# A hybrid pool-mixer and mLSTM block: right sums of the output projections made one pass earlier and in place, first operands of the projections split inside the mLSTM, weight loads separated from their split, head norm in groups of two tiles

## The chip, the cores and the metric

The kernel runs on one core of one Trainium2 chip. A core has a matrix engine (TensorE, PE in the profile; PEld is its weight load), VectorE (DVE), ScalarE (ACT), GpSimd (POOL) and SyncE (SP), which issues most of the transfers. Each engine takes its instructions in the order of the program. Times are device microseconds of one execution; before the change the median of three runs is 3157.75 us (3157.44 to 3160.65).

## The reference

Everything is float32; the sequence has 4096 rows, and D_MODEL, both groups' widths and the output are 1024 columns wide.

```python
def reference(x, norm_w, w_in, ...):
    u = rmsnorm(x, norm_w[l])
    proj = u @ w_in[l]                       # 1024 x 5120
    pool_x, pool_z, m_x, m_z, m_o = ...      # five slices of 1024
    y_pool = pool_mixer(pool_x, pool_w[l], pool_scale[l]) * jax.nn.silu(pool_z)
    y_mlstm = mlstm_branch(m_x, m_z, m_o, ...)
    mixed = jnp.concatenate([y_pool, y_mlstm], axis=-1)
    x = x + mixed @ w_out[l]                 # 2048 x 1024
    return rmsnorm(x, final_norm_w)

def mlstm_branch(mx, mz, mo, ...):
    xc = jax.nn.silu(causal_conv(mx, conv_w, conv_b))
    ...                                      # q, k, v maps, gates, chunkwise mLSTM of 4 heads
    h = jax.nn.sigmoid(mo) * h
    mu = jnp.mean(h, axis=-1, keepdims=True)             # per head, 256 columns
    var = jnp.mean(jnp.square(h - mu), axis=-1, keepdims=True)
    hn = ((h - mu) * lax.rsqrt(var + EPS)).reshape(B, S, 1024) * mh_norm_w
    return (hn + m_skip * xc) * jax.nn.silu(mz)
```

## The kernel before, in words

Every float32 product is made from two halves: `split` (L110, L111) writes a rounded high part with ACT and the rest with DVE, and `mm3` (L117, L118, L119) multiplies high by high, high by low and low by high.

**Phase A** (0 to 752.7 us) normalises 8 blocks of 512 rows, writes the result to memory (`us_d`), projects pool_x and pool_z, and writes the pool mixer's output (`yp_d`). Between the blocks' steps, at the steps that `JOBS_AT` names, `sums` (L493 loads, four POOL operations, L497 stores) makes the left sums of `us_d` and `yp_d` that phase C needs. The last pair for `yp_d` runs after the loop.

**Phase B** (to 1758.1 us) is the mLSTM, 32 chunks of 128 rows, steps ordered by the text `ORDER`. It first loads and splits its weights `wm` (L127 through two buffers `ws`) and the block-diagonal maps (L623), then for each two chunks `project` loads u (L700), casts it (L702), takes the low part (L703) and multiplies; the front part of a chunk begins with L740. Its steady state is a pair of chunks in 58.05 us. When nothing is left to project, `next_weights` takes that place: it loads and splits the right operands of the first four products of phase C.

**Phase C** is four passes driven by `drive`: pass 1 `o1` (pool output times upper half of w_out, plus x, to `r_d`), pass 2 `mo` (output gate, head norm, then 256 transposes L1069 to `hs_d`), pass 3 `mz` (the mz gate times `hs_d`, to `ym_d`), pass 4 `o2` (`ym_d` times the lower half of w_out, plus `r_d`, and the final norm). A pass works on 4 row blocks of 1024 rows. Each block is 7 products of half-size matrices in place of 8, from sums of quarters of the left and of the right matrix (Strassen's scheme in Winograd's form), each product in two steps of 24 matmuls of 128 by 512: 56 steps a pass. The seven results chain through sums in PSUM and in tiles named `ch`.

What sets the order around the change:

- Left operands: ACT's queue issues their load three steps ahead (tile `sr`), and they are split two steps ahead on ACT and DVE (`make`).
- Right operands: seven slots per pass. `Pass.load` loads and splits one; in the last row block of a pass the next pass's slots are loaded, each directly at the step where the old slot is free. The sums of quarters among them (`SUM_OF`) come from memory, where `Pass.stage` has put them (5 tiles, POOL) during earlier passes: those of passes 2 and 3 in pass 1, those of pass 4 in pass 3. For pass 1 they are made while loading (`load_right`, L129 on POOL).
- Transposes: `Head.done` normalises one tile of 128 rows by 512 columns (two heads): DVE statistics, POOL power (L1038), DVE bias (L1040), ACT scaling (L1043). The groups of four tiles are transposed at the steps that `FREE_BANKS` names, after which L1071 on DVE evicts the bank.
- Left sums of pass 4: when the last of a block's four results is there, `put_sums` (L201, L203, L205, L209 on POOL) and deferred stores (L196 on SP) follow. Pass 4's additions to `r_d` load it with L980.
- The program reuses eight completion counters in turn for transfers, so that a transfer also waits until the one eight places ahead, from SP or ACT, has landed.

## Time and profile before

| | us |
|---|---|
| median of three runs | 3157.75 |
| profiled execution, its own time | 3153.02 |
| its span, first to last instruction | 3151.3 |
| phase A | 752.7 |
| phase B, with its entry | 1005.4 |
| phase C | 1393.2 |

The page gives busy time and share of each engine, the span in 40 slices, the transfers, the chain that ended last and the costliest groups. A stretch table gives the same busy times for chosen stretches, with the clock that TensorE was granted (1.00 is full), the share of time that the 16 DMA engines were busy, and GB/s. A group's row ends with the idle time of its engine just before it and the operation that ended it. The table of waits for TensorE names that operation for every gap, with the sum, the number and the longest. Numbers in brackets with x count instructions.

### The profile page before, as it was taken

Reading aid. Unit: us, or ns where it says so; the run is one execution under the profiler, and the core shown is the slowest. Engines: PE = TensorE matmul, PEld = TensorE weight load, DVE = VectorE, ACT = ScalarE, POOL = GpSimd, SP = SyncE. Lnnn points to the kernel's source line nnn. Section 1 sums busy time; section 2 is a strip of 40 time slices with the busy share of each in tenths; the row PEclk is TensorE's granted clock in tenths of the full one; section 3 lists DMA queues with packets and bytes.
Section 4 is the critical chain, followed back from the end, with each engine's and each line's share of the span. In section 5 each row is a group of like instructions: output and inputs, shape, how many; then the busy total and the mean of one; then the engine's idle time right before and its main releaser. Section 6 shows DMA issues by size and latency. Waiting matters only on the chain. (4 is left out here: it accounts for less than half of the span.)

```text
span 3151.3 us, 45085 instructions
## 1 busy us (share of the span) xinstructions
PE 2919.7 (93%) x15912; PEld 2522.1 (80%) x15912; DVE 2089.8 (66%) x4160; ACT 1373.6 (44%) x2727; POOL 960.7 (30%) x1015
## 2 busy tenths in 40 slices
...
GB/s 211 124 153 159 155 181 184 184 174 201 46 64 51 48 68 48 61 55 51 61 58 111 227 309 268 238 225 192 209 218 230 260 273 302 260 290 208 213 208 157
DMA packets 256419, 530.55 MB, mean 168 GB/s; under 512 B 28352, under 2 KB 71872, under 8 KB 256192
## 3 DMA queue, kind: packets, MB, share of 16 engines
...
q14 instruction: 102, 0.84, 0.1%
...
## 5 line engine op out<-in xcount | busy, mean ns | idle before, releaser
L117 PE MATMUL acc<-u,w 128*128 128x512 f32 (+1 forms) x2016 | 691.6, 343 | 2.2 <-ACT u L110 1.8
L119 PE MATMUL acc<-u,w 128*128 128x512 f32 (+1 forms) x2016 | 682.4, 339 | 0.0
L118 PE MATMUL acc<-u,w 128*128 128x512 f32 (+1 forms) x2016 | 680.7, 338 | 0.0
L117 PE MATMUL ps<-w,sr 128*128 128x512 f32 x1344 | 536.7, 399 | 44.4 <-ACT sr L110 29.6
L119 PE MATMUL ps<-w,sr 128*128 128x512 f32 x1344 | 533.6, 397 | 9.2 <-DVE sr L111 9.0
L118 PE MATMUL ps<-w,sr 128*128 128x512 f32 x1344 | 532.5, 396 | 0.0
L111 DVE TENSOR_TENSOR sr<-sr 128x1024 fp32r<-128x1024 f32 x224 | 293.5, 1314 | 304.3 <-ACT sr L110 299.4
L110 ACT CAST sr<-sr 128x1024 fp32r<-128x1024 f32 x224 | 234.2, 1048 | 552.0 <-PE ps L118 293.6
L117 PEld LDWEIGHTS acc<-u,w 128*128 128x128 f32 x2016 | 383.7, 190 | 44.3 <-ACT u L110 2.5
L118 PEld LDWEIGHTS acc<-u,w 128*128 128x128 f32 x2016 | 383.7, 190 | 40.3
L119 PEld LDWEIGHTS acc<-u,w 128*128 128x128 f32 x2016 | 383.5, 190 | 40.2
L117 PEld LDWEIGHTS ps<-w,sr 128*128 128x128 f32 x1344 | 257.9, 192 | 99.6 <-ACT sr L110 32.3
L119 PEld LDWEIGHTS ps<-w,sr 128*128 128x128 f32 x1344 | 257.1, 191 | 69.5 <-DVE sr L111 16.7
L118 PEld LDWEIGHTS ps<-w,sr 128*128 128x128 f32 x1344 | 257.6, 192 | 53.5 <-issue 0.5
L656 DVE SCALAR_TENSOR_TENSOR xc<-mx,col,xc 128x256 f32<-128x256 f32 x384 | 221.2, 632 | 55.4 <-POOL mx L715 46.4
L644 POOL TENSOR_TENSOR cs<-c,cs 128x516 fp32r<-128x516 f32 x124 | 176.4, 1422 | 204.2 <-ACT cs L643 181.7
L1038 POOL TENSOR_TENSOR rs<-rs,nhalf 128x2 f32<-128x2 f32 x64 | 56.0, 876 | 521.0 <-DVE mv L1035 325.9
L117 PE MATMUL ps<-sr,w 128*128 128x512 f32 x448 | 176.5, 394 | 4.3 <-ACT sr L110 3.3
L118 PE MATMUL ps<-sr,w 128*128 128x512 f32 x448 | 176.0, 393 | 1.4 <-DVE sr L111 1.4
L119 PE MATMUL ps<-sr,w 128*128 128x512 f32 x448 | 175.7, 392 | 0.0
L867 PE MATMUL mm<-va,st 128*128 128x258 f32 x384 | 85.6, 318 | 64.2 <-DVE st L111 42.6
L322 DVE TENSOR_TENSOR ch<-ps,ch 128x512 f32<-128x512 f32 x192 | 127.2, 681 | 14.4 <-PE ps L119 13.6
...
## 6 DMA issues: line engine op xcount, KB each, us to landing
sr<-us_d ACTq DMA_DIRECT2D x112, 512.0 KB, 5.0
...
```

The lines of the kernel that those rows point to most:

```text
L110: nc.scalar.copy(out=hi, in_=raw)
L111: (eng or nc.vector).tensor_tensor(out=lo, in0=raw, in1=hi.bitcast(F32), op=ALU.subtract)
L117: nc.tensor.matmul(ps, lhsT=a[0], rhs=b[0], start=start and k == 0, stop=False, skip_group_check=skip)
L118: nc.tensor.matmul(ps, lhsT=a[0], rhs=b[1], start=False, stop=False, skip_group_check=skip)
L119: nc.tensor.matmul(ps, lhsT=a[1], rhs=b[0], start=False, stop=stop and k == n - 1, skip_group_check=skip)
L322: nc.vector.tensor_tensor(out=v(t), in0=ps, in1=v(t), op=ALU.add)
L644: nc.gpsimd.tensor_tensor(out=t[:, 1], in0=cst[h], in1=t[:, 0].bitcast(F32), op=ALU.subtract)
L656: nc.vector.scalar_tensor_tensor(out=a[:, t], in0=m[:, t, i:i + TB], scalar=conv_w[:, jj * 4 + i:jj * 4 + i + 1], in1=a[:, t], op0=ALU.mul ...
L867: nc.tensor.matmul(nps, lhsT=wt[:, w, h, :], rhs=vh[v], start=i == 0, stop=first and i == 2)
L1038: nc.gpsimd.tensor_tensor(out=rs, in0=rs, in1=nhalf[:, 0:2], op=ALU.pow)
```

## The change

The change does these things:

- **Right sums.** `Pass.stage` becomes `put_right_sums`: the four sums are formed in place in the four loaded tiles, and each is stored as it is made. They are made one pass ahead: those of pass 1 in phase A (`right_sums`, in place of the last block's left-sum jobs), those of passes 2, 3 and 4 in passes 1, 2 and 3. All four sums of every pass now come from memory; `load_right` goes.
- **Phase A's end.** The last left sums of `yp_d` move into pass 1 (`last_sums`).
- **Entry to phase B.** The pools `stp` and `wsp` are opened in A and again in B, so that the `ws` buffers in B lie where A's other tiles were; the maps are loaded in six pieces into `xu` tiles.
- **First operands.** `next_operands` replaces `next_weights` (11 steps for 17): slots 0 to 3 of pass 1, and the left operands of the first three steps of pass 1, which `drive` gets as `first`.
- **Loads and splits of slots.** `fetch` issues loads into separate tiles ahead, `load` those into the slot itself, and the split is deferred to after the next step.
- **Head norm.** Mean, variance, power and bias are taken over two tiles at a time; `FREE_BANKS` names other steps and counts; up to 4 of the skip loads are outstanding (3 before).
- **Left sums of pass 4.** Three of the four are made when block a21 is ready, deferred, one of them on DVE; only s4 is left for a12.
- Pool sizes (`ch` 20 to 18 tiles; `x` 8 and `u` 12 tiles become 12 `xu` tiles in both phases; the junk tiles 2 to 1), and the final norm's weights are loaded in pass 4 in two halves.

```diff
+B_OF = ((0, 0), None, (1, 0), None, None, None, (1, 1))
 SUM_OF = (None, 1, None, 2, 0, 3, None)
-FREE_BANKS = {6: 2, 7: 2, 11: 3, 12: 3, 13: 3, 0: 3, 1: 2}
+FREE_BANKS = {7: 4, 12: 4, 13: 3, 0: 1, 1: 4}
 AHEAD = 4
 NORM_AT = ((2, 3, 5), (3, 4, 6))
-JOBS_AT = ((0, 2), (0, 2, 6))
+JOBS_AT = ((0, 2), (0, 2, 4, 6))
...
+        def get_right(self, dst, k, n, kh, ch):
+            rows, c0 = self.sources[ch]
+            for i in range(n):
+                nc.sync.dma_start(out=dst[:, i] if n > 1 else dst, in_=rows(k + i + 4 * kh)[:, c0:c0 + T])
+        def put_right_sums(self, q, k, put=None):
+            put = put or (lambda dst, t: nc.sync.dma_start(out=dst, in_=t))
             b11, b12, b21, b22 = q[0, 0], q[0, 1], q[1, 0], q[1, 1]
-            nc.gpsimd.tensor_tensor(out=t3, in0=b22, in1=b12, op=ALU.subtract)
             nc.gpsimd.tensor_tensor(out=b12, in0=b12, in1=b11, op=ALU.subtract)
+            put(self.sums[0][:, k, :], b12)
             nc.gpsimd.tensor_tensor(out=b22, in0=b22, in1=b12, op=ALU.subtract)
+            put(self.sums[1][:, k, :], b22)
+            nc.gpsimd.tensor_tensor(out=b11, in0=b22, in1=b11, op=ALU.subtract)
+            put(self.sums[2][:, k, :], b11)
             nc.gpsimd.tensor_tensor(out=b21, in0=b21, in1=b22, op=ALU.subtract)
-            yield
-            for i, t in enumerate((b12, b22, t3, b21)):
-                nc.sync.dma_start(out=self.sums[i][:, k, :], in_=t)
-        def load(self, i, pool, tag, tile):
+            put(self.sums[3][:, k, :], b21)
...
+        def fetch(self, i, tile):
+            if SUM_OF[i] is None:
+                (kh, ch), self.raws = B_OF[i], [tile() for _ in range(4)]
+                rows, c0 = self.sources[ch]
+                for k in range(4):
+                    nc.sync.dma_start(out=self.raws[k], in_=rows(k + 4 * kh)[:, c0:c0 + T])
+        def load(self, i, pool, tag):
...
             self.slots[i] = hi, lo = [pool.tile([P, 4, T], F32R, name=tag) for _ in range(2)]
...
+            if SUM_OF[i] is not None:
+                for k in (0, 2):
+                    nc.sync.dma_start(out=lo[:, k:k + 2].bitcast(F32), in_=self.sums[SUM_OF[i]][:, k:k + 2, :])
+                return [lambda k=k: split(lo[:, k:k + 2].bitcast(F32), hi[:, k:k + 2], lo[:, k:k + 2])
+                        for k in (0, 2)]
+            raws = self.raws
+            return [lambda k=k: split(raws[k], hi[:, k], lo[:, k]) for k in range(4)]
...
         def load(p, i):
-            for _ in p.load(i, *slot_pool(i), tile):
-                pass
+            def splits(todo):
+                for f in todo:
+                    f()
+            todo = p.load(i, *slot_pool(i))
+            defer(lambda: splits(todo))
...
+        for t, pairs in enumerate(first):
+            got[t] = tuple([pair[v] for pair in pairs] for v in range(2))
...
             if n + r == 0:
                 miss = [v for v in range(NP) if v not in p.slots]
-                if miss and miss[0] <= t // 2 + 4:
+                if miss:
+                    p.fetch(miss[0], tile)
                     load(p, miss[0])
...
             if r + 1 == NR and n + 1 < len(passes):
                 if kh == 0 and i:
                     load(passes[n + 1], i - 1)
+                if kh == 1 and i < NP - 1 or (kh, i) == (0, NP - 1):
+                    passes[n + 1].fetch(i, tile)
...
             if b + 1 == NB:
-                jobs.append((yp_d[b // 2], 0))
+                jobs += [(p_out1, k) for k in (0, 2)]
...
+    xu = ctx.enter_context(tc.tile_pool(name="xu", bufs=12))
+    with tc.tile_pool(name="b_mx", bufs=NJ) as mxp, \
+            tc.tile_pool(name="b_one", bufs=1) as one, \
+            tc.tile_pool(name="b_st", bufs=4) as stp, \
+            tc.tile_pool(name="b_ws", bufs=2) as wsp, \
...
             for k in range(4):
-                load_right(*wm[i], k, ((1, i % 2, i // 2),), halves(in_rows, 2 * D), ws_tile)
+                raw = ws_tile()
+                r0, c0 = (k + 4 * (i % 2)) * P, 2 * D + i // 2 * T
+                nc.sync.dma_start(out=raw, in_=w_in[r0:r0 + P, c0:c0 + T])
+                split(raw, wm[i][0][:, k], wm[i][1][:, k])
...
+        def next_operands():
             for i in range(4):
-                yield from p_out1.load(i, w1p, "w1", u_tile)
+                p_out1.fetch(i, x_tile)
+                todo = p_out1.load(i, w1p, "w1")
+                yield
+                for n, f in enumerate(todo):
+                    f()
+                    if n == 1 and len(todo) > 2:
+                        yield
+            for t in range(AHEAD - 1):
+                pairs = []
+                for k in range(2):
+                    hi, lo = x_tile(F32R), x_tile(F32R)
+                    nc.sync.dma_start(out=lo.bitcast(F32), in_=yp_d[0][t // 2][:, 2 * (t % 2) + k, :])
+                    pairs.append((hi, lo))
+                first.append(pairs)
+            yield
+            for pairs in first:
+                for hi, lo in pairs:
+                    split(lo.bitcast(F32), hi, lo)
+                yield
...
-                mv = wk.tile([P, 2, 2], F32, name="mv")
+                if self.q == 0:
+                    group[0] = wk.tile([P, 4, 2, 2], F32, name="mv"), []
+                mv, ts = group[0]
+                ts.append(t)
...
+                    nc.vector.bn_aggr(out=mv[:, self.q, hh, :], in_=stats[:, hh, :])
+                if self.q % 2 == 0:
                     return
-                rh, ch = {2: (0, 0), 4: (1, 1), 5: (1, 0), 6: (0, 1)}[i]
-                name = {2: "c11", 4: "u3", 5: "s1", 6: "u2"}[i]
-                hn = [getattr(it, name) for it in self.items]
-                return [self.turned(r, rh, ch, hn, jj) for jj in range(4)]
-            def turned(self, r, rh, ch, hn, jj):
+                two = slice(self.q - 1, self.q + 1)
+                rs = wk.tile([P, 2, 2], F32, name="rs")
+                nc.vector.tensor_single_scalar(out=rs, in_=mv[:, two, :, 1], scalar=4 * EPS, op=ALU.add)
+                nc.gpsimd.tensor_tensor(out=rs, in0=rs, in1=nhalf.rearrange("p (a b) -> p a b", a=2), op=ALU.pow)
+                nb = wk.tile([P, 2, 2], F32, name="nb")
+                nc.vector.scalar_tensor_tensor(out=nb, in0=mv[:, two, :, 0], scalar=-1.0, in1=rs,
+                                               op0=ALU.mult, op1=ALU.mult)
+                for q in range(2):
+                    for hh in range(2):
+                        hw = ts[self.q - 1 + q][:, hh * DH:(hh + 1) * DH]
+                        nc.scalar.activation(out=hw, in_=hw, func=AF.Identity, scale=rs[:, q, hh:hh + 1],
+                                             bias=nb[:, q, hh:hh + 1])
...
+                if name == "a21":
+                    c11, u3 = self.c11, self.u3
+                    def sums():
+                        s1, self.s2 = x_tile(), x_tile()
+                        nc.gpsimd.tensor_tensor(out=s1, in0=t, in1=u3, op=ALU.add)
+                        put("s1", s1)
+                        nc.vector.tensor_tensor(out=t, in0=c11, in1=t, op=ALU.subtract)
+                        put("s3", t)
+                        nc.gpsimd.tensor_tensor(out=self.s2, in0=s1, in1=c11, op=ALU.subtract)
+                        put("s2", self.s2)
+                    defer(sums)
+                elif name == "a12":
+                    s4 = x_tile()
+                    nc.gpsimd.tensor_tensor(out=s4, in0=t, in1=self.s2, op=ALU.subtract)
+                    put("s4", s4)
...
+        def last_sums():
+            for k in range(4):
+                q = {}
+                for name in ("a11", "a12", "a21", "a22"):
+                    q[name] = x_tile()
+                    nc.sync.dma_start(out=q[name], in_=yp_d[-1][A_OF.index(name)][:, k, :])
+                yield
+                put_sums(yp_d[-1], k, q["a11"], q["a12"], q["a21"], q["a22"], x_tile, nc.gpsimd, store)
+                yield
...
+            if (n, r) == (0, 1) and m in (1, 3, 5, 7, 9, 11) or (n, r) == (0, 2) and m in (1, 3):
+                next(more)
+            if n < 3 and m in (((2, 5, 8, 11), (), (6, 9, 11, 13), ()) if n == 0 else
+                               ((1, 4, 7, 10), (1, 4), (1, 4), ()))[r]:
+                next(weights[n])
+            if (n, r, m) == (3, 0, 2):
+                for h in range(2):
+                    fw.append(x_tile())
+                    nc.sync.dma_start(out=fw[h], in_=final_w[:, h * T:(h + 1) * T].partition_broadcast(P))
+        drive(order, ring, slot_pool, x_tile, psp, background, first)
```

Three places in the order of the program.

**SP at the entry to phase B, before.** Names: `st` and `yp_d` are the left sums' tiles and memory, `ws` the mLSTM weights' buffers, `u<-us_d` the loads for `project`.

```order
L620 DMA ws<-in_w_if_dram 128x24x8
L623 DMA bvg<-in_qkv_cols_dram 128x8x128
L560 DMA yp_d_79<-sg 128x512
L700 DMA u<-us_d_72 128x2x256
L1157 DMA fw<-in_final_w_dram 128x1024
L493 DMA st<-yp_d_79 128x1024 x3
L497 DMA yp_d_79<-st 128x1024 x2
L700 DMA u<-us_d_72 128x2x256
L497 DMA yp_d_79<-st 128x1024 x2
L623 DMA st<-in_qkv_cols_dram 128x1024 x3
L700 DMA u<-us_d_72 128x2x256 x4
```

**The same place after.** `xu<-us_d` is the load of u now, `xu<-in_qkv_cols_dram` that of the maps.

```order
L568 DMA yp_d_79<-sg 128x512 x3
L605 DMA ws<-in_w_in_dram 128x512 x2
L568 DMA yp_d_79<-sg 128x512
L626 DMA bif<-in_b_if_dram 128x8
L634 DMA xu<-in_w_if_dram 128x24x8
L638 DMA xu<-in_qkv_cols_dram 128x512
L605 DMA ws<-in_w_in_dram 128x512
L638 DMA xu<-in_qkv_cols_dram 128x512
L605 DMA ws<-in_w_in_dram 128x512
L638 DMA xu<-in_qkv_cols_dram 128x512 x2
L605 DMA ws<-in_w_in_dram 128x512
L638 DMA xu<-in_qkv_cols_dram 128x512
```

The sums' loads and stores are gone, and the weight loads, which stood in phase A, now follow its last stores, mixed with those of the maps; the loads of u follow further on.

**PE in the first row block of pass 2, before.** `ps<-ident,ch` are the transposes of the head norm's tiles, `ps<-w,sr` the matmuls of a step.

```order
L119 MATMUL ps<-w_21061,sr 128x512
L1069 MATMUL ps<-ident,ch 128x128 x4
L117 MATMUL ps<-w_21061,sr 128x512
L118 MATMUL ps<-w_21062,sr 128x512
L119 MATMUL ps<-w_21061,sr 128x512
L117 MATMUL ps<-w_21061,sr 128x512
L118 MATMUL ps<-w_21062,sr 128x512
L1069 MATMUL ps<-ident,ch 128x128 x2
L119 MATMUL ps<-w_21061,sr 128x512
L117 MATMUL ps<-w_21061,sr 128x512
L118 MATMUL ps<-w_21062,sr 128x512
```

**The same block after** (the three lines of `mm3` are L111, L112, L113 there).

```order
L113 MATMUL ps<-w_20972,sr 128x512
L111 MATMUL ps<-w_20972,sr 128x512
L112 MATMUL ps<-w_20973,sr 128x512
L113 MATMUL ps<-w_20972,sr 128x512
L1109 MATMUL ps<-ident,ch 128x128 x16
L111 MATMUL ps<-w_21046,sr 128x512
L112 MATMUL ps<-w_21047,sr 128x512
L113 MATMUL ps<-w_21046,sr 128x512
```

Transposes stood in pieces of two and four within the step after the result; now sixteen stand together between two steps, the first of them two steps after their result.

**SP between pass 3 and pass 4, before.** `ym_d_83` holds the left operands of pass 4's last row block, `x<-in_w_out_dram` are raw right operands, `ch<-r_d` is what pass 4 adds.

```order
L196 DMA ym_d_83<-x 128x512
L196 DMA ym_d_83<-ch 128x512
L196 DMA ym_d_83<-x 128x512 x2
L127 DMA x<-in_w_out_dram 128x512 x4
L980 DMA ch<-r_d 128x512 x13
L196 DMA out_dram<-ch 128x512 x6
```

**The same place after.** `xu` tiles hold left sums in the stores, and raw right operands or the final norm's weights in the loads.

```order
L184 DMA ym_d_83<-xu 128x512
L184 DMA ym_d_83<-ch 128x512
L184 DMA ym_d_83<-xu 128x512
L1011 DMA ch<-r_d 128x512 x14
L1242 DMA xu<-in_final_w_dram 128x512 x2
L1011 DMA ch<-r_d 128x512 x2
L184 DMA out_dram<-ch 128x512 x2
```

The raw loads of the last slot, which stood between the stores and the loads of r, now stand further up, ahead of the last four pairs of stores; the loads of r follow the stores directly, with the final norm's weights behind fourteen of them.

186 lines of the change are left out of this document (75 added, 111 removed).

## The prediction

> **What bounds the kernel now.** I read the page first, then a table of stretches cut at the stage borders, then what TensorE waits for in each stretch.
>
> ```profile
> PE 2919.7 (93%) x15912; PEld 2522.1 (80%) x15912; DVE 2089.8 (66%) x4160; ACT 1373.6 (44%) x2727; POOL 960.7 (30%) x1015
> ...
> core 0: us, PE busy (x) PEld busy (x) DVE busy (x) ACT busy (x) POOL busy (x), PEclk, DMA share, GB/s
> 0.00:752.70 752.70, 736.26 (x3232) 608.11 (x3232) 424.64 (x582) 183.34 (x319) 209.81 (x207) 1.00 0.48 169
> 752.70:820.85 68.15, 42.19 (x256) 40.72 (x257) 17.33 (x39) 18.77 (x51) 18.73 (x22) 0.67 0.45 147
> 820.85:1689.50 868.65, 800.90 (x6486) 777.41 (x6485) 704.35 (x1948) 608.83 (x1477) 414.31 (x524) 0.97 0.18 59
> 1689.50:1758.13 68.63, 49.30 (x310) 45.78 (x308) 55.24 (x142) 41.09 (x103) 36.86 (x39) 0.81 0.25 81
> 1758.13:1770.93 12.80, 0.00 (x0) 0.00 (x0) 0.49 (x4) 1.56 (x3) 2.52 (x2) 0.58 0.78 261
> 1770.93:1962.79 191.86, 166.86 (x672) 131.49 (x673) 94.68 (x111) 37.02 (x41) 71.22 (x46) 0.93 0.88 299
> 1962.79:2115.11 152.32, 152.32 (x673) 126.13 (x672) 88.58 (x113) 38.34 (x41) 0.00 (x0) 1.00 0.71 233
> 2115.11:2495.65 380.54, 350.44 (x1585) 282.73 (x1583) 273.24 (x637) 217.14 (x335) 52.08 (x60) 0.96 0.66 219
> 2495.65:2815.92 320.27, 312.54 (x1361) 256.11 (x1361) 208.23 (x247) 123.56 (x168) 112.95 (x71) 0.99 0.84 283
> 2815.92:3151.30 335.38, 308.93 (x1345) 253.66 (x1343) 222.98 (x343) 103.94 (x193) 42.19 (x46) 0.96 0.58 200
> ```
>
> TensorE is the bound wherever it is fed. The row 1962.79:2115.11 is that state: 673 matmuls of 512 columns in 152.32 us, 0.2263 us each, clock 1.00. Two of a pass's four row blocks are one such stretch, so an unhindered pass is 304.6. Against that the table shows where time is lost: the entry to the mLSTM (68.15 us, clock 0.67), its last chunks (68.63 us, clock 0.81), an empty 12.80 us, the first half of pass 1 of the projections (191.86 for 152.32), the second pass, the third, and the start of the fourth. What TensorE waited for there, in the order of these stretches:
>
> ```profile
> PE mm L117 <- ACT u L702: 22.2, 3, 14.4
> ...
> PE ps L117 <- ACT sr L110: 12.8, 1, 12.8
> ...
> PE ps L117 <- ACT sr L110: 29.6, 4, 12.8
> ...
> PE ps L1069 <- ACT ch L1043: 16.2, 14, 3.0
> ...
> PE ps L117 <- DVE ch L989: 14.5, 1, 14.5
> ```
>
> Each row is total, times, longest; 29.6 contains the 12.8. So the change has waits to work on, and none of them is a lack of matmul speed. Phase A (752.70 us at clock 1.00) and the periodic mLSTM (820.85 to 1689.50) keep their instruction sequence per block, so I put both at 0.
>
> **The entry to the mLSTM.** The transition before:
>
> ```profile
> 761.30 0.42 SPq L700 DMA_DIRECT2D u<-us_d  x1
> ...
> 765.87 1.27 SPq L493 DMA_DIRECT2D st<-yp_d  x3
> 766.08 0.22 POOL L734 MEMSET va<- 128x8 f32 x4 [4.28 <-DMA u<-us_d]
> 766.44 0.62 ACT L702 CAST u<-u 128x512 fp32r<-128x512 f32 x1 [6.64 <-DMA u<-us_d]
> 767.11 0.29 PEld L117 LDWEIGHTS mm<-u,w 128*128 128x128 f32 x1 [14.85 <-ACT u L702]
> ...
> L110 ACT CAST w<-ws x14: 617/621/626, 702.0 to 757.4; 128x512 fp32r<-128x512 f32 x14
> L111 DVE TENSOR_TENSOR w<-ws,w x14: 676/691/1022, 702.7 to 758.0; 128x512 fp32r<-128x512 f32 x14
> ...
> DMA to landing us min/median/max: 2.5/3.6/6.0
> ```
>
> Only one u load goes out at 761.30; the rest stand on SP behind the last left sums (L493 at 765.87 and their stores), and the first front matmul comes at 820.85. The change takes those sums away, but it also puts all 16 mLSTM weight loads behind the end of phase A: their two buffers now lie where phase A's weights were. In the rows, 14 of these casts run from 702.0 to 757.4 beside phase A, nearly free. After, a buffer turns round in landing 3.6 + cast 0.62 + split 0.69 + about 0.3 to issue = 5.2 us; eight rounds of two are 42 us, so the last split is at 752.7+42 = 795. About 73 of the 192 project matmuls (256 columns, half of 0.2263 = 0.113) then remain: 8 us, front at 803, **gain 17**. With the shortest landing (2.5) the round is 4.1, front at 794, gain 27. With 6.0 it is 7.6, the end 752.7+61+8 = 822, gain -1; q/k/v and u loads crowd the same stretch, so I keep -5 to 27 and take 17, by the median landing.
>
> **The last chunks.** The operands of pass 1 are split here in both kernels.
>
> ```profile
> L111 DVE TENSOR_TENSOR w<-u,w 128x512 fp32r<-128x512 f32 x11 | 11.6, 1055 | 0.1
> ...
> L129 POOL TENSOR_TENSOR u<-u 128x512 f32<-128x512 f32 x6 | 8.9, 1494 | 2.8 <-DMA u<-in_w_out_dram 2.8
> ```
>
> The 12 POOL additions go (slots 1 and 3 come summed from memory), which frees 8.9 us of POOL in this window and, as the DVE split beside them took 1055 against 691 ns alone, 11 x 0.36 = 4.0 us of DVE. Six left operands are new: 6 x (0.62 ACT + 0.69 DVE), 4.1 us of DVE, work that before stood behind 1758.13. DVE (55.24 of 68.63) is the engine nearest to full here, so its load hardly changes; the POOL waits shorten. **Gain 5**, between -2 (the added splits lie on the chain) and 12 (all 8.9 of POOL and part of the DVE time come out).
>
> **Start and first half of pass 1.**
>
> ```profile
> 1770.93:1853.81 82.88, 80.22 (x336) 64.83 (x337) 52.61 (x59) 21.29 (x26) 40.02 (x26) 0.96 0.91 319
> 1853.81:1962.79 108.98, 86.64 (x337) 66.66 (x336) 42.07 (x52) 15.73 (x15) 31.20 (x21) 0.91 0.86 283
> ...
> 1760.26:1777.32 17.06, 6.35 (x14) 4.56 (x15) 5.66 (x5) 4.69 (x7) 5.48 (x4) 0.50 0.94 324
> ```
>
> From 1758.13 to 1962.79 are 204.66 us for 152.32 of matmuls. Three steps' left operands are ready when the mLSTM ends, so the 12.80 us and the half clock behind them go. What is late next is transfer: the rows show 0.86 to 0.91 of the DMA engines busy and 283 to 319 GB/s. The bytes issued ahead of the last left operand of this half, counted in program order, are 57.4 MB before and 51.5 after (pass 3's right sums leave, phase A's last left sums enter). Over 204.66 us the rows moved 3.3 + 26.4 + 30.8 = 60.5 MB, 296 GB/s; 5.9 MB at that rate are **20 us**. Everything hidden would be 52; bytes bunched at the start, where pass 1's loads of x, the last three weight slots and the first sums all go out on SP, could leave 8. Also, in the new order DVE's weight split for slot 4 stands ahead of the left split of step 4, and waits for its load: a stall of some 4 us, inside the 20. Range 8 to 38.
>
> The Trainium skill, "TensorE: Matmul & The Clock Gate", Part 1 on the HAM clock gate, says that an idle window of about 3.4 us halves the clock and a busy one of that length restores it. The 17.06 us at 0.50 above are five such windows, so the trace agrees. It speaks against a remaining 4 us stall: by the rule that costs up to 1.7 us more, and the 20 would be 18.3.
>
> **Pass 2 (gate and head norm).**
>
> ```profile
> L1069 PE MATMUL ps<-ident,ch 128*128 128x128 f32 x240 | 44.4, 297 | 29.4 <-ACT ch L1043 16.2 <-ACT sr L110 4.2 <-DVE mv L1035 2.9
> L1038 POOL TENSOR_TENSOR rs<-rs,nhalf 128x2 f32<-128x2 f32 x60 | 52.1, 868 | 508.4 <-DVE mv L1035 323.4 <-DVE rs L1037 173.9 <-ACT x L1062 11.1
> ...
> 2199.16 1.03 PE L1069 MATMUL ps<-ident,ch 128*128 128x128 f32 x8
> ```
>
> Eight transposes span 1.03 us, the last of them 0.27, so one follows another by 0.109: 240 take 26 us. 380.54 - 304.6 - 26 leaves 50 us lost, of which 29.4 is idle time directly before transposes and the rest is clock (0.96) and gaps that the profile gives to PE's pipeline. The chain from result to transpose (DVE statistics, POOL power 868 ns, DVE bias, ACT scaling) now has two steps, 2 x 24 x 0.2263 = 10.9 us, where it had none or one, and the power comes half as often. Against it: a transpose bank four results later may still be read by DVE, and pass 3's right sums (8.4 MB) enter, for about 87 MB in the pass, 250 GB/s, less than the 319 shown. I leave 17 of the 50: **gain 33**, 15 (half the idle only) to 42.
>
> **Pass 3 and the start of pass 4.**
>
> ```profile
> 2842.26 1.22 POOL ch L205
> 2843.48 1.23 POOL x L209
> 2845.10 0.44 SPq L127
> ...
> 2847.41 0.43 SPq L980
> ...
> 2848.36 4.86 DMA ch<-r_d
> ...
> 2856.18 0.69 DVE ch L989
> 2856.92 0.80 PE ps L117
> ```
>
> Pass 3 lost 320.27 - 304.6 - 17 x 0.109 = 14 us; weight splits now stand behind the step instead of ahead of the next left split on ACT, and two of its waits were for that split. Pass 4's right sums enter here too. **Gain 6**, 0 to 12. In pass 4 the chain of waits runs from the left sums (16 POOL operations, 1.2 to 2.2 us) through SP's stores to the loads of r, issued only at 2847.41, and DVE's addition at 2856.18. Now three of the four sums of a tile are made a block earlier and only s4 remains, so these loads go out about 6 us into pass 4, some 25 us before. By 6 + 16 issues of 0.43 + landing 4.9 + additions, the last needed sum is at 22 to 25 us, against a need at 21.8 (four steps of 24 x 0.2263). The first quarter lost 95.54 - 76.16 = 19.4; I leave 5: **gain 14**, 4 to 18.
>
> **Sum.** 17 + 5 + 20 + 33 + 6 + 14 = 95. The profiled execution (span 3151.3) took 3153.0, so 3058; the median of the runs shown, 3157.75, lies 4.7 above it. I forecast 3060, between. All low ends together are a gain of 20, all high ends 149; independent deviations from 95 add to about 29 either way.
>
> **Rivals.**
> 1. *Transfer takes the first half of pass 1 and spills on.* For it: 0.86 to 0.91 DMA share. Against: fewer bytes. The 20 becomes 0 and pass 2 gains 15: 3060 + 20 + 18 = **3098**. The Trainium skill, "DMA: Bandwidth & Descriptors", section "Issuing engines are not separate DMA queues", says that loads from SP and ACT share 16 engines and interleave; by it SP's bunched sums push back ACT's left loads, which is this case. No run here shows it yet.
> 2. *Weight loads replace SP's wait at the entry.* For it: two buffers and 6.0 us landings. Against: the median 3.6. 3060 + 17 + 5 = **3082**.
> 3. *The change does not do what it says in pass 2*: the transposes wait for banks or loads instead of the norm, gain 0. For it: of the 29.4 only 16.2 are for L1043's scaling. **3093**.
> 4. *Slower: left loads queue behind the sums.* SP's stores of sums wait for POOL, and the program reuses eight completion counters in turn, so that a transfer waits for the one eight places ahead; if ACT's left loads stall on these, each row block costs what 1853.81:1962.79 cost, 32.8 over 76.16. Six blocks (pass 1's first two and pass 2) stand to lose. Now they and the start lose 12.8 + 39.5 + 50 = 102, and the other gains are 42. So it decides from 144 / 32.8 = 4.4 blocks; with all six, 197, the time is 3157 + 197 - 144 = **3210**. Against: blocks three and four of pass 1 ran clean at 233 GB/s.
>
> **How the numbers follow.** Forecast 0.66, rivals 0.12, 0.08, 0.06; rival 4 0.05; the remaining 0.03 is a mix of small losses near no change. 0.2% of the median, about what a measurement of this kernel can tell from no change, is 6.3 us. Forecast and rivals 1 to 3 (0.92) are faster, less 0.02 for several of them together, which would be no change; the mix is split 0.02 to no change and 0.01 to slower. So faster 0.90, same 0.04, slower 0.06. The range 3015 to 3110 holds the forecast with its 29 and a little correlation, and rivals 1 to 3; it leaves out rival 4 and the ends.
>
> **What would show it.** Right: front at about 803; no empty stretch where the 12.80 us stood; DMA share still near 0.9 with 165 to 185 us for the first half of pass 1; waits of L1069's successor under 8 us; pass 4's first gap under 5 us. Wrong: the last weight split past 810; left splits on ACT waiting over 10 us in pass 2; transposes waiting for DVE's evictions; a periodic mLSTM pair other than 58.05 us.

## The result, and the profile after

The changed kernel takes 3121.76 us (median of four runs, 3114.22 to 3122.14); the kernel before beside it takes 3157.6 us (four runs, 3156.61 to 3160.65). The ratio is 0.9879, 95% interval 0.9862 to 0.9896: faster by 36 us, or 1.2%. The forecast was 3060, 98 us faster, with a range that ended at 3110. The direction was right, the size was not.

The page of the changed kernel begins with the engines' busy time, their share and their number of instructions:

```profile
PE 2916.4 (93%) x15912; PEld 2527.6 (81%) x15912; DVE 2103.1 (67%) x4107; ACT 1371.2 (44%) x2722; POOL 897.8 (29%) x955
```

POOL lost 60 operations and DVE 53, and yet DVE is busy 13 us longer than before. The stretch table of the changed kernel, cut at the borders of the same stages (same columns; only the border inside the mLSTM lies 33 matmuls later in the program than in the table of before):

```profile
0.00:751.89 751.89, 735.54 (x3232) 608.29 (x3232) 430.90 (x571) 175.90 (x305) 218.46 (x211) 1.00 0.49 170
751.89:809.60 57.71, 40.95 (x257) 39.33 (x258) 24.58 (x49) 26.09 (x64) 9.73 (x18) 0.73 0.52 152
809.60:1682.20 872.60, 812.55 (x6519) 790.05 (x6518) 704.56 (x1955) 613.68 (x1487) 409.30 (x519) 0.96 0.18 58
1682.20:1746.60 64.40, 42.87 (x279) 38.88 (x277) 51.47 (x140) 40.42 (x98) 26.45 (x32) 0.81 0.21 66
1746.60:1934.16 187.56, 162.83 (x673) 130.47 (x673) 90.23 (x104) 34.95 (x35) 47.58 (x32) 0.93 0.87 295
1934.16:2086.48 152.32, 152.32 (x674) 126.13 (x672) 90.35 (x114) 40.81 (x45) 6.09 (x4) 1.00 0.77 249
2086.48:2461.75 375.27, 345.16 (x1578) 284.34 (x1576) 265.38 (x573) 207.37 (x327) 51.58 (x42) 0.97 0.72 236
2461.75:2785.41 323.66, 313.62 (x1369) 255.68 (x1368) 215.45 (x258) 123.41 (x171) 86.72 (x56) 0.99 0.82 277
2785.41:2879.90 94.49, 81.58 (x338) 65.51 (x336) 67.65 (x85) 28.66 (x44) 23.13 (x15) 0.93 0.67 219
2879.90:3109.14 229.24, 228.99 (x1009) 188.87 (x1007) 155.10 (x249) 76.55 (x141) 17.14 (x25) 1.00 0.59 201
```

Behind the last row come 11.06 us without a matmul (11.2 before). The profiled execution has a span of 3120.2 us, 31.1 less than before. Set against the table of before, stage by stage (the mLSTM is divided at the front of chunk 30, counted from 1, at 1658.7 before and 1653.5 after):

| stage | before, us | after, us | gain | forecast |
|---|---|---|---|---|
| start to the first front (phase A, entry) | 820.85 | 809.60 | 11.2 | 17 |
| steady mLSTM, to the front of chunk 30 | 837.9 | 843.9 | -6.1 | 0 |
| last chunks | 99.4 | 93.1 | 6.3 | 5 |
| start and first half of pass 1 | 204.66 | 187.56 | 17.1 | 20 |
| second half of pass 1 | 152.32 | 152.32 | 0 | 0 |
| pass 2 | 380.54 | 375.27 | 5.3 | 33 |
| pass 3 | 320.27 | 323.66 | -3.4 | 6 |
| first block of pass 4 | 95.54 | 94.49 | 1.1 | 14 |
| the rest of pass 4, and the tail | 239.8 | 240.3 | -0.5 | 0 |

Unrounded, the gains add to 31.1, the terms of the forecast to 95. Of the 64 missing, 28 lie in pass 2, 22 in pass 3 and the start of pass 4, and 6 each in the steady mLSTM and at the entry. The two rows of the mLSTM depend on where it is divided: at the border of the prediction's own row, 1689.50, whose next matmul in the program stands at 1678.7 after, the steady part is 0.3 us longer and the last chunks are 0.6 shorter. What TensorE waits for, from the tables of waits of the changed kernel for these stretches (total, times, longest), in the order entry, first half of pass 1, pass 2, and last the first block of pass 4:

```profile
PE map L643 <- DMA xu<-in_qkv_cols_dram: 12.2, 1, 12.2
...
PE ps L111 <- ACT sr L104: 18.5, 4, 14.7
...
PE ps L1109 <- ACT ch L1084: 24.0, 13, 6.2
...
PE ps L113 <- DVE sr L105: 8.6, 1, 8.6
PE ps L111 <- DVE ch L1020: 4.3, 4, 3.2
```

L1109, L1084 and L1020 are the transposes, the head norm's scaling and the addition of r, which were L1069, L1043 and L989. The wait for r fell from 14.5 to 4.3, as foretold; the wait of the transposes for the scaling *rose*, from 16.2 to 24.0.

For pass 2 it helps to see where in a block the time goes. A block has 14 steps, counted from 0. A step's loss is its time less 24 x 0.2263 = 5.43 us, and less 0.1075 us for each transpose in it. Over the four blocks the losses add to 50.1 us before and 45.6 after. After, they stand at step 13 (16.8), step 7 (12.1), step 1 (7.7), step 0 (5.8) and step 8 (2.1). That is behind the two groups of results of a block, and gave two theories of pass 2, which the experiments below take apart:

- **W, work.** DVE has more to do from about step 10 of a block to step 1 of the next than fits there, since three results follow each other; two steps' distance then buys nothing.
- **P, queue.** The scaling is late because the power stands in POOL's queue behind the sums that were moved into this pass.
- Rivals: **A**, the skip loads that ACT waits for (the tiles of `xc_d` that are added to the head norm's result); **G**, the group of two tiles; **E**, the order of DVE's evictions (W is a rival of each).

Theory P has a place in the trace. POOL in order of time after the second block's end at 2270.65 (start, us):

```profile
2275.40 1.44 POOL L1077 TENSOR_TENSOR rs<-rs,nhalf 128x4 f32<-128x4 f32 x1 [7.48 <-DVE mv L1071]
2279.61 1.28 POOL L138 TENSOR_TENSOR xu<-xu 128x512 f32<-128x512 f32 x1 [2.78 <-DMA xu<-in_w_in_dram]
2280.98 2.22 POOL L140 TENSOR_TENSOR xu<-xu 128x512 f32<-128x512 f32 x1
2283.27 1.28 POOL L143 TENSOR_TENSOR xu<-xu 128x512 f32<-128x512 f32 x1
2284.51 1.26 POOL L145 TENSOR_TENSOR xu<-xu 128x512 f32<-128x512 f32 x1
2285.73 1.01 POOL L1077 TENSOR_TENSOR rs<-rs,nhalf 128x4 f32<-128x4 f32 x1
```

The power L1077 was asked for at about 2281 and runs at 2285.73, behind four right sums of pass 3. What that does further on, in the timeline of ACT of the same kernel:

```profile
2286.97 0.60 ACT L1084 ACTIVATE ch<-ch,nb,rs 128x256 f32<-128x256 f32 x1 [6.88 <-DVE nb L1079]
```

ACT sat idle 6.88 us for the bias of two tiles, and TensorE waited 3.05 us for this scaling. Its longest wait for a scaling, 6.2, is of another kind. At the first block's end POOL is free and the bias is there at 2173.3, but the scaling runs only at 2176.01: it stands in ACT's queue behind a skip tile whose load is late, which is theory A's case:

```profile
2174.87 0.72 ACT L1102 ACTIVATE xu<-xu,col 128x512 f32<-128x512 f32 x1 [4.34 <-DMA xu<-xc_d]
```

### The profile page after: what moved, and what is told of

Its sections match the earlier page's. It is cut to its first block, busy times and chain, and to the rows that moved or that the text cites. A ratio compares the mean times of both kernels' runs of the same rounds, so it can differ in the third digit from the quotient of the medians.

```text
span 3120.2 us, 44964 instructions
## 1 busy us (share of the span) xinstructions
PE 2916.4 (93%) x15912; PEld 2527.6 (81%) x15912; DVE 2103.1 (67%) x4107; ACT 1371.2 (44%) x2722; POOL 897.8 (29%) x955
## 3 DMA queue, kind: packets, MB, share of 16 engines
q10 hardware_dynamic: 31824, 115.88, 12.1%
## 5 line engine op out<-in xcount | busy, mean ns | idle before, releaser
L111 PE MATMUL ps<-w,sr 128*128 128x512 f32 x1320 | 524.1, 397 | 28.0 <-ACT sr L104 19.6
L113 PE MATMUL ps<-w,sr 128*128 128x512 f32 x1320 | 520.4, 395 | 15.1 <-DVE sr L105 15.0
L112 PE MATMUL ps<-w,sr 128*128 128x512 f32 x1320 | 521.3, 395 | 0.0
L105 DVE TENSOR_TENSOR sr<-sr 128x1024 fp32r<-128x1024 f32 x221 | 285.6, 1295 | 299.8 <-ACT sr L104 298.8
L104 ACT CAST sr<-sr 128x1024 fp32r<-128x1024 f32 x221 | 231.1, 1048 | 529.2 <-PE ps L112 274.3
L111 PE MATMUL acc<-u,w 128*128 128x512 f32 x1024 | 398.8, 390 | 1.5 <-ACT u L104 1.5
L112 PE MATMUL acc<-u,w 128*128 128x512 f32 x1024 | 398.8, 389 | 0.0
L113 PE MATMUL acc<-u,w 128*128 128x512 f32 x1024 | 398.6, 389 | 0.0
L111 PEld LDWEIGHTS ps<-w,sr 128*128 128x128 f32 x1320 | 252.5, 191 | 84.4 <-ACT sr L104 21.7
L113 PEld LDWEIGHTS ps<-w,sr 128*128 128x128 f32 x1320 | 251.5, 191 | 71.6 <-DVE sr L105 19.1
L111 PE MATMUL acc<-xu,w 128*128 128x256 f32 x992 | 295.7, 298 | 0.0
L112 PEld LDWEIGHTS ps<-w,sr 128*128 128x128 f32 x1320 | 252.2, 191 | 52.8 <-issue 0.7
L113 PE MATMUL acc<-xu,w 128*128 128x256 f32 x992 | 287.2, 290 | 0.0
L112 PE MATMUL acc<-xu,w 128*128 128x256 f32 x992 | 284.4, 287 | 0.0
L673 DVE SCALAR_TENSOR_TENSOR xc<-mx,col,xc 128x256 f32<-128x256 f32 x384 | 221.6, 633 | 13.1 <-ACT xc L755 11.5
L111 PEld LDWEIGHTS acc<-u,w 128*128 128x128 f32 x1024 | 192.1, 188 | 42.3 <-ACT u L104 2.2
L113 PEld LDWEIGHTS acc<-u,w 128*128 128x128 f32 x1024 | 192.2, 188 | 40.2
L112 PEld LDWEIGHTS acc<-u,w 128*128 128x128 f32 x1024 | 192.2, 188 | 40.1
L111 PEld LDWEIGHTS acc<-xu,w 128*128 128x128 f32 x992 | 194.0, 196 | 1.2
L112 PEld LDWEIGHTS acc<-xu,w 128*128 128x128 f32 x992 | 194.1, 196 | 0.1
L113 PEld LDWEIGHTS acc<-xu,w 128*128 128x128 f32 x992 | 193.8, 195 | 0.0
```

Of the source, the lines that this page charges most:

```text
L104: nc.scalar.copy(out=hi, in_=raw)
L105: (eng or nc.vector).tensor_tensor(out=lo, in0=raw, in1=hi.bitcast(F32), op=ALU.subtract)
L111: nc.tensor.matmul(ps, lhsT=a[0], rhs=b[0], start=start and k == 0, stop=False, skip_group_check=skip)
L112: nc.tensor.matmul(ps, lhsT=a[0], rhs=b[1], start=False, stop=False, skip_group_check=skip)
L113: nc.tensor.matmul(ps, lhsT=a[1], rhs=b[0], start=False, stop=stop and k == n - 1, skip_group_check=skip)
L673: nc.vector.scalar_tensor_tensor(out=a[:, t], in0=m[:, t, i:i + TB], scalar=conv_w[:, jj * 4 + i:jj * 4 + i + 1], in1=a[:, t], op0=ALU.mul ...
```

## The experiments

A kernel that was run once is read by its stages and not by its total, since four runs of the changed kernel lie 8 us apart. Stages vary too: among the kernels whose edit leaves it alone, pass 2 took 375.1 to 381.5 us (five profiles, the longest being that of the run with all sums on DVE), and pass 3 with the first block of pass 4 took 416.9 to 421.4 (nine). Smaller differences than these say nothing. Each diff is against the changed kernel unless it says otherwise.

### Pass 2: loads, queue, or work

**The skip loads (theory A).** In the changed kernel ACT scales a skip tile (L1102) one step before its use, and in pass 2 it idles 33 us in front of these for their load. Moved to directly ahead of the transposes:

```diff
-                    defer(lambda: nc.scalar.activation(out=sk, in_=sk, func=AF.Copy, scale=msk[:, j:j + 1]))
...
                     sk, = got
+                    nc.scalar.activation(out=sk, in_=sk, func=AF.Copy, scale=msk[:, j:j + 1])
```

> ACT's scaling of the skip tile stands directly ahead of the transposes that use it, instead of one step after its load was issued. Theory A: on ACT this operation waits for the load (33 us of idle ACT in pass 2) with head norm's tanh and scaling queued behind it. Then pass 2 falls by 8 to 15 us from 375.3, the waits at the last step of a block go from 3.5 to 6.8 us each to under 2. Theory P says 0 to 4 us, since the powers behind the sums on POOL stay late.

Measured: pass 2 376.2 us against 375.27, span 3117.1. Theory A's forecast failed, but the edit did not take the wait away: ACT still idles 26.0 us in front of the skip tiles for their load (33.1 in the changed kernel), and at the first block's end it still stands ahead of the scalings:

```profile
2172.77 0.72 ACT L1106 ACTIVATE xu<-xu,col 128x512 f32<-128x512 f32 x1 [4.82 <-DMA xu<-xc_d]
```

What these loads cost therefore stays open.

**The sums out of pass 2 (theory P).** Pass 3's right sums are made at the end of pass 1 instead:

```diff
-            if n < 3 and m in (((2, 5, 8, 11), (), (6, 9, 11, 13), ()) if n == 0 else
+            if n in (0, 2) and m in (((2, 5, 8, 11), (), (6, 9, 11, 13), ()) if n == 0 else
...
+            if (n, r) == (0, 3) and m in (0, 2, 4, 6, 8, 10, 12, 13):
+                next(weights[1])
```

> The right sums of pass 3 are made in the last row block of pass 1 and no longer in pass 2; everything else is the changed kernel. Theory P (POOL's queue): in pass 2 the four POOL operations of a sums job (6.1 us) stand ahead of a power of the head norm, and transposes wait for it. Then pass 2 (375.3 us in the changed kernel) falls by 8 to 14 us, TensorE's wait for the scaling (24.0 us) to 10 to 16, and no wait of 3 us stays at the fourth step after a block's last result. Rival A (ACT's queue, the skip loads): pass 2 stays within 3 us. Rival G (grouping over two tiles alone): pass 2 stays within 3 us. Pass 1 may get up to 5 us longer, its last block was clean at 76.2.

Measured: pass 2 took 366.1 us, 9.2 less, and the loss of step 1 went from 7.7 to 0. So theory P holds, and it is worth 9 of the missing 28. But pass 1 paid: SP ran ahead of the row block, three of the four sets of sums were added between 1911 and 1960 us, a left operand came 6.0 us late, and pass 1's third block took 88.33 us in place of 76.14, a price of 12 where 5 were expected. The span, 3121.2, is that of the changed kernel. Of the waits for the scaling, 17.3 us are left in pass 2, where 10 to 16 were expected: theory P is not all.

**The group of two tiles (theory G).** On top of the edit before, the head norm of before, tile by tile:

```diff
-                if self.q % 2 == 0:
-                    return
-                two = slice(self.q - 1, self.q + 1)
-                rs = wk.tile([P, 2, 2], F32, name="rs")
...
+                rs = wk.tile([P, 2], F32, name="rs")
+                nc.vector.tensor_single_scalar(out=rs, in_=mv[:, :, 1], scalar=4 * EPS, op=ALU.add)
+                nc.gpsimd.tensor_tensor(out=rs, in0=rs, in1=nhalf[:, 0:2], op=ALU.pow)
```

> The right sums of pass 3 are made in pass 1, and the head norm goes tile by tile as before the change, with the changed steps for the transposes. Against the run with the early right sums alone (pass 2: 366.1, of it 14.7 lost at the last step of the blocks and 8.1 at the eighth). Theory G (grouping over two tiles delays the last pair: its tanh on ACT stands behind four scalings that wait for the first pair's power): pass 2 falls by 5 to 12 us, the losses at the last step to under 2 each. Rival W (the work of the chain itself on DVE, ACT and POOL is what takes over two steps): pass 2 stays within 3 us or gets longer by up to 8, since POOL has 64 powers of 0.87 us in place of 32 of 1.06.

Measured: pass 2 367.3 us against 366.1. The loss of step 13 fell from 14.7 to 10.1 and that of step 1 rose from 0 to 10.1. Grouping is worth about a microsecond here, either way; theory G falls, and the wait only changed its place.

**Other steps for the transposes (theory E).** On top of the early sums:

```diff
-FREE_BANKS = {7: 4, 12: 4, 13: 3, 0: 1, 1: 4}
+FREE_BANKS = {7: 4, 12: 4, 0: 4, 1: 4}
```

> The right sums of pass 3 are made in pass 1, and the transposes of a block's sixth product stand three steps after its result in place of two and three (four at the first step of the next block, none at the last). Theory W (the chain needs over two steps, 10.9 us, but under three): the loss at the last step (14.7 us over the pass) goes, the one at the first step of a block (5.7) falls too, pass 2 goes from 366.1 to 346 to 352. Rival E (evictions: eight transposes' banks in two steps wait for DVE): 5 to 12 us come back at the first three steps, pass 2 stays at 356 to 366.

Measured: pass 2 362.7 us, inside the range of theory E, but not for its reason. Theory W was put here as a matter of distance (the chain from a result to its transposes needs more than two steps and less than three), and with its 346 to 352 it missed as well. Step 13 went from 14.7 to 0.5, step 0 from 5.7 to 0.9, and step 1 from 0 to 17.3. TensorE's waits in pass 2 of this run:

```profile
PE ps L1109 <- ACT ch L1084: 13.1, 9, 3.2
PE ps L111 <- DVE xu L1111: 3.4, 3, 1.3
```

Evictions (L1111) are 3.4 us of it; 13.1 is still the scaling. Again the wait moved and did not go. The stretch table of this run around the border of two blocks, and the whole pass, shows why:

```profile
2097.36:2460.07 362.71, 340.84 (x1569) 282.30 (x1568) 261.35 (x569) 206.77 (x324) 31.77 (x30) 0.98 0.67 225
...
2254.40:2290.00 35.60, 31.58 (x156) 26.21 (x155) 30.25 (x74) 25.41 (x45) 4.56 (x5) 0.96 0.68 223
```

Over the pass DVE, the third of the engines in a row, is busy 261.35 of 362.71 us, 72%. Over the 35.60 us around the border it is busy 30.25, 85%, though it is also waiting for POOL's powers in there. Three results need DVE there one after another, each four tiles with an addition (0.68 us), the gate (0.68), two statistics (0.41 each), their two aggregates (0.17 each) and one eviction (0.74): 4 x 3.26 = 13.0 us for each result. Two splits of 1.2 us come with it, and the two steps of a result last 10.9 us. This is theory W as a matter of work, still only argued at this point.

**Less work for DVE (theory W).** On top of the last edit the statistics of a tile are taken from its first head alone and used for both, so that half of the head norm's statistics are left out; the chain has the same steps otherwise:

```diff
-                for hh in range(2):
-                    nc.vector.bn_stats(out=stats[:, hh, :], in_=t[:, hh * DH:(hh + 1) * DH])
-                    nc.vector.bn_aggr(out=mv[:, self.q, hh, :], in_=stats[:, hh, :])
+                nc.vector.bn_stats(out=stats[:, 0, :], in_=t[:, 0:DH])
+                for hh in range(2):
+                    nc.vector.bn_aggr(out=mv[:, self.q, hh, :], in_=stats[:, 0, :])
```

> As the run with early right sums and later transposes (pass 2: 362.7, of it 34.0 lost), but the head norm takes both heads' statistics from the first head's half of a tile: one of two statistics operations of a tile (0.41 us on DVE) is left out. Theory W (DVE is full from the tenth step of a block to the second of the next: three results of 4 x 3.3 us each and two splits of 1.2 us in two steps of 10.9): 1.6 us less DVE work a result, with three results in a row that is up to 5 us a block, so pass 2 falls by 8 to 15 us. Rival L (the latencies of ACT's and POOL's steps in the chain, with DVE waiting): pass 2 falls by under 4 us.

Measured, pass 2 in the stretch table:

```profile
2095.94:2438.82 342.88, 334.69 (x1570) 277.87 (x1568) 242.21 (x510) 206.18 (x323) 34.87 (x30) 0.99 0.72 239
```

DVE is busy 19.1 us less (261.35 to 242.21), and the pass is 19.8 us shorter; the losses fell from 34.0 to 14.2. That is more than theory W's 8 to 15, and far over the 4 that was put down for rival L, the latencies of ACT's and POOL's steps. DVE's work, at an average share of 72%, thus set the time of this pass nearly microsecond for microsecond. One thing the run does not separate: the statistics also stand in the chain from a result to its transposes, 4 x 0.41 = 1.6 us a result or 26 us for the 16 of the pass. Whether the time goes because DVE is full there, or because its part of the chain is shorter, is not shown; around the border it was idle for 15% of the time.

**The sums at other steps.** Theory P's gain without its price: the sums stay in pass 2, and only their steps change, to those where no head norm runs.

```diff
-                               ((1, 4, 7, 10), (1, 4), (1, 4), ()))[r]:
+                               ((1, 4, 7, 10), (1, 4), (1, 4), ()) if n == 2 else
+                               ((0, 1, 2, 3), (3, 5), (3, 5), ()))[r]:
```

> The right sums of pass 3 stay in pass 2, but are loaded and added two steps later in a block (from the fourth step, in the first block from the first), so that on POOL they stand behind all powers of the block before and ahead of those of the next. Theory P (order on POOL): pass 2 falls by 5 to 11 us from 375.3, the loss at the second step of the blocks (7.7 us over the pass) goes under 2, the one at the eighth step of the first block (3.3) too, and pass 1 stays as in the changed kernel. If it was the work itself on POOL (contention with DVE): pass 2 stays within 3 us.

Measured: pass 2 366.9 us, 8.4 less; the loss of step 1 is 0.7 (7.7) and that of step 7 in the first block 0 (3.3). So the work may stay in the pass, only not at those steps. (The sums' place in POOL's queue and their place beside DVE's head norm move together here; the trace above shows the queue.) One set of sums runs ahead into pass 1, whose last block pays 4.2 us (80.39 against 76.18), though it was expected to stay as it was. Span 3115.9.

### Pass 3 and the start of pass 4: which engine adds the left sums

The trace of the changed kernel at the first step of pass 4, DVE in order of time, shows the 8.6 us wait's other end:

```profile
2786.50 3.42 DVE L1159 TENSOR_TENSOR ch<-ch 128x512 f32<-128x512 f32 x2
2791.07 0.69 DVE L1159 TENSOR_TENSOR ch<-ch 128x512 f32<-128x512 f32 x1 [1.15 <-POOL xu L1157]
2791.68 1.75 DVE L1143 TENSOR_TENSOR ch<-ch,xu 128x512 f32<-128x512 f32 x1
2793.36 1.21 DVE L105 TENSOR_TENSOR sr<-sr 128x1024 fp32r<-128x1024 f32 x1
```

The left split L105, for which TensorE waits, stands on DVE behind s3 (L1159), which waits for POOL's s1 (L1157). And DVE's additions take 1.71 us each (3.42 for two) or 1.75, not 0.69. POOL at the same time:

```profile
2789.34 1.71 POOL L1157 TENSOR_TENSOR xu<-ch 128x512 f32<-128x512 f32 x1
2791.12 1.77 POOL L1161 TENSOR_TENSOR xu<-xu,ch 128x512 f32<-128x512 f32 x1
```

Theory **D** said that s3 is too much for DVE, and belongs back on POOL. Its rival **C** said that the two engines hinder each other, so that all of the sums should stand on one.

**s3 back to POOL.**

```diff
-                        nc.vector.tensor_tensor(out=t, in0=c11, in1=t, op=ALU.subtract)
+                        nc.gpsimd.tensor_tensor(out=t, in0=c11, in1=t, op=ALU.subtract)
```

> The left sum s3 of pass 4 goes back from DVE to POOL, still a block earlier. Theory D (DVE's queue): the four s3 operations on DVE wait for s1 on POOL and hold up the split of the left operand behind them, the 8.6 us at the start of pass 4. Then this wait falls under 3 us, the first block of pass 4 from 94.5 to 86 to 90, pass 3 by 1 to 4. Rival C (sharing between DVE and POOL): DVE's operations stay slow (1.7 us in place of 0.7) as long as POOL adds, POOL now adds longer, and the wait stays at 5 to 10 us.

Measured, pass 3 and the first block of pass 4:

```profile
2463.65:2793.37 329.72, 317.73 (x1370) 258.07 (x1368) 210.04 (x246) 124.13 (x173) 109.68 (x69) 0.98 0.83 272
2793.37:2893.65 100.28, 86.03 (x338) 67.19 (x336) 65.04 (x80) 28.04 (x43) 27.79 (x18) 0.91 0.62 204
```

Pass 3 is 6.1 us longer and the block 5.8, together 430.0, clear of the 416.9 to 421.4 of the kernels that leave them alone. Theory D falls; the change's own step of giving s3 to DVE was worth about 12 us, by this one run. It was a good step, taken one third of the way.

**All three sums on DVE.**

```diff
-                        nc.gpsimd.tensor_tensor(out=s1, in0=t, in1=u3, op=ALU.add)
+                        nc.vector.tensor_tensor(out=s1, in0=t, in1=u3, op=ALU.add)
...
-                        nc.gpsimd.tensor_tensor(out=self.s2, in0=s1, in1=c11, op=ALU.subtract)
+                        nc.vector.tensor_tensor(out=self.s2, in0=s1, in1=c11, op=ALU.subtract)
```

> The three left sums of pass 4 that are made early (s1, s3, s2) all run on DVE; only s4 stays on POOL. Theory C (while POOL adds, DVE's operations take 1.7 us in place of 0.7, and s3 waits for s1 across engines): 12 operations of 0.69 us on DVE are 8.3 us a block and nothing slows, so the first step of pass 4 loses under 5 us where the changed kernel lost 11.5, and the first block falls from 94.5 to 85 to 89. Theory D (DVE's queue is too full there whatever POOL does): the loss at this step stays at 8 to 13, and pass 3 gets 3 to 8 us longer as the splits of left operands stand behind more sums.

Measured, the same two stretches:

```profile
2464.48:2779.78 315.30, 310.62 (x1370) 255.68 (x1369) 207.58 (x282) 125.03 (x172) 53.31 (x30) 0.99 0.85 285
2779.78:2871.74 91.96, 80.53 (x338) 64.40 (x337) 66.22 (x92) 28.96 (x44) 11.00 (x8) 0.96 0.67 221
```

Pass 3 is 8.4 us shorter, the block 2.5, together 407.3, clear of the other kernels on the other side. In pass 3 DVE does 24 operations more than in the changed kernel and is busy 7.9 us *less* (207.58 against 215.45). DVE in order of time at the first step of pass 4:

```profile
2785.53 0.68 DVE L1159 TENSOR_TENSOR ch<-ch 128x512 f32<-128x512 f32 x1
2786.13 0.68 DVE L1161 TENSOR_TENSOR xu<-xu,ch 128x512 f32<-128x512 f32 x1
2787.34 1.22 DVE L105 TENSOR_TENSOR sr<-sr 128x1024 fp32r<-128x1024 f32 x1
```

Each sum takes 0.68 us. Rival C is right in both places: pass 3 is shorter, and the loss of pass 4's first step fell from 11.5 (9.1 to 11.8 in the kernels that leave it alone) to 2.0. The block missed the 85 to 89 that C expected, since a new loss of 7.2 stands at its third step, where a split waits on DVE, which has no pause from 2776 to 2799.

### The entry and the mLSTM: more weight buffers

**Eight buffers.** The weights of the mLSTM turn round in two buffers; here they have eight, four of `ws` and four of phase B's `st`:

```diff
-            tc.tile_pool(name="b_ws", bufs=2) as wsp, \
+            tc.tile_pool(name="b_ws", bufs=4) as wsp, \
...
-                raw = ws_tile()
+                raw = ws_tile() if k % 2 else st()[:, 0:T]
```

> The 16 loads of the mLSTM weights use eight buffers instead of two, and go out at once at the end of phase A. Theory B (two buffers make the entry long): the last split falls from 800.7 to 785 to 790 and the first front matmul from 809.6 to 793 to 800. Rival Q (the maps' loads and ACT's copies of the maps bound it, TensorE waits 12.2 us for the first map): the front stays within 4 us of 809.6, or gets later because the maps' loads now stand behind all 16.

Measured: the last weight split ends at 772.4 us in place of 800.7, sooner than the 785 to 790 expected, and yet the first front comes at 816.4, *later* than with two buffers (809.6). The first wait of the maps is longer:

```profile
PE map L643 <- DMA xu<-in_qkv_cols_dram: 21.9, 1, 21.9
```

The turn-round of the buffers was not what bounded the entry. What was left as a suspect is that the loads of the maps stand behind those of the weights (Q), so the next run put them ahead.

**Eight buffers, maps first.** Against the last kernel, the loop that loads and splits the weights moves behind the loads of the maps:

```diff
-        for i in range(4):
-            for k in range(4):
-                raw = ws_tile() if k % 2 else st()[:, 0:T]
...
+        for i in range(4):
+            for k in range(4):
+                raw = ws_tile() if k % 2 else st()[:, 0:T]
```

> Eight buffers for the 16 loads of the mLSTM weights, and the loads of the maps stand ahead of them. Theory Q (the entry is the sum of the maps' load, ACT's copies of the maps, and the loads of u, which need the maps' tiles): the first map matmul comes 3 to 5 us sooner than 764.1 and the front at 795 to 804 in place of 809.6 (changed kernel) and 816.4 (eight buffers, weights first). Rival T (transfer: 8.8 MB in the stretch bound it): the front stays at 806 to 817.

Measured: the first map matmul comes 2.5 us sooner than in the changed kernel, but the front stands at 814.39 us, still later than with two buffers. Theory Q falls, for what TensorE now waits for longest at the entry is something else:

```profile
PE mm L111 <- ACT xu L735: 12.9, 1, 12.9
PE map L642 <- DMA xu<-in_qkv_cols_dram: 9.5, 1, 9.5
```

ACT of this run in order of time:

```profile
786.80 0.62 ACT L104 CAST w<-ws 128x512 fp32r<-128x512 f32 x1
787.61 3.58 ACT L735 CAST xu<-xu 128x512 fp32r<-128x512 f32 x5 [0.19 <-DMA xu<-us_d]
```

The casts of u (L735, which is L736 in the changed kernel) begin only when all weights are cast, and their loads, which SP issues behind those of the weights, landed no sooner (the first at 787.58); the 192 matmuls of `project` begin only then. With two buffers the casts of u stand between those of the weights, from 779.27 on, and the matmuls fill that time. The front lies where a bound by transfer (T) was to show, but the DMA share at the entry was 0.46, so it is the order of the transfers that shows, and not their volume.

**The mLSTM in the same runs.** Pairs of chunks as stretches, in the kernel before, then in the changed one (two of its pairs), then with eight buffers:

```profile
1253.13:1311.19 58.06, 54.09 (x442) 52.58 (x441) 47.46 (x133) 41.19 (x101) 28.50 (x37) 0.97 0.17 57
```

```profile
1067.91:1127.60 59.69, 55.83 (x443) 54.37 (x442) 47.60 (x133) 41.28 (x101) 28.52 (x37) 0.94 0.17 52
1127.60:1186.01 58.41, 54.57 (x443) 53.12 (x442) 47.52 (x133) 41.20 (x101) 28.48 (x37) 0.97 0.17 57
```

```profile
1128.05:1186.16 58.11, 53.39 (x443) 51.70 (x442) 49.03 (x133) 41.27 (x100) 27.98 (x37) 1.00 0.18 56
```

The column to read is the clock, ahead of the DMA share. TensorE pauses once in a pair, for 2.85 us before and 2.77 to 2.80 after. In all three kernels the clock changes only at points of a fixed grid of 3.413 us, whatever the program does. A mean of 0.97 over 58 us is one window at half speed, and 0.94 is two (1 - 0.5 x 6.83 / 59.69 = 0.943). The kernel before came to sit on this grid: 17 windows are 58.02 us, its pairs are 58.01 to 58.06 from the eighth on, and from there the half window came at the same place in each, 32.7 us behind the front. In the changed kernel a pair is longer by some 0.1 us at the same place, slides along the grid by 0.37 us a pair at 58.4, and when the pause reaches the border of two windows, both are halved and the pair takes 59.7. That happened twice and cost 3.2 of the 6.1 us that the steady mLSTM lost; the rest are pairs of 58.2 to 58.4. The loss itself varies: nine other kernels with the same mLSTM have two such pairs each and took 837.9 to 843.7 us for this stretch, where the changed kernel took 843.9 and the kernel before 837.9.

With eight buffers the pause is divided into 1.05 and 2.00 us, no window there is halved, and the pair is still 58.1: then the chain from chunk to chunk bounds it, not TensorE. The two other kernels with eight buffers pause in the same way, but have three such half windows and one. What decides is how much of the pauses falls into one window: in the steady mLSTM of all fourteen profiles (900 to 1640 us), each window at full clock in which TensorE was idle for 1.96 us or more was followed by a half one, 144 in number, and none in which it was idle for 1.76 or less.

Where the first 0.1 us comes from was not settled. The Trainium skill, "TensorE: Matmul & The Clock Gate", Part 1 on the HAM clock gate, gives the window as free-running and 3413 ns long; these traces agree (3.413 us). They do not bear out the prediction's reading that a window must be idle for the whole 3.4 us: 1.96 us were enough.

### Together

**Sums at other steps, and left sums on DVE.** The other steps for pass 3's right sums and all three left sums on DVE, both edits in one kernel.

> The two edits that helped, together: the right sums of pass 3 two steps later, and the left sums s1, s3, s2 of pass 4 on DVE. If the two causes are separate, the gains add: 8.4 us (measured for the left sums) and 5 to 11, so 3101 to 3108 against 3120.2 of the changed kernel's span. If they are not, it stays above 3110.

Measured: 3104.71 us (median of four runs, 3101.52 to 3107.40) against 3154.91 of the kernel before on the same chip (seven runs); the ratio is 0.9843, interval 0.9828 to 0.9858. The interval ends below that of the changed kernel (0.9862 to 0.9896), so this version beats both. Its pass 2, pass 3 and first block of pass 4:

```profile
2087.44:2453.08 365.64, 341.03 (x1578) 281.73 (x1577) 263.63 (x573) 207.15 (x327) 45.96 (x38) 0.98 0.72 238
2453.08:2768.18 315.10, 310.45 (x1369) 255.93 (x1368) 208.12 (x283) 125.70 (x173) 53.00 (x30) 0.99 0.86 286
2768.18:2860.11 91.93, 82.09 (x338) 65.23 (x336) 65.18 (x91) 28.15 (x43) 10.94 (x8) 0.94 0.69 220
```

They are 9.6, 8.6 and 2.6 us shorter than in the changed kernel: the two gains add, as they must if they have different causes. The last block of pass 1 pays 5.0 again.

**The same with eight buffers.**

> As the run before, with eight buffers for the loads of the mLSTM weights, where the mLSTM ran without half-clock windows and pass 1 began 4.6 us sooner (1742.0 in place of 1746.6) though the front came 6.8 us later. If that gain is the mLSTM's own, it adds: 3096 to 3105. If the later passes lose it again by another order of transfers (pass 3 and 4 lost 7 us there), it is within 3 us of the run before.

Measured: 3104.41 us (3099.74 to 3110.46), ratio 0.9843, interval 0.9822 to 0.9865: no difference. The front comes at 813.66, pass 1 begins at 1740.24 (1742.65 in the kernel beside it), and nothing of these 2.4 us is left at the end: pass 2 is 2.7 us longer and pass 3 3.5. Ten kernels without the eight buffers begin pass 1 between 1742.65 and 1747.94, so a gain of this size is hardly one.

## Why the prediction was right or wrong

- **The entry (17; measured 11.2).** The numbers came close, the last weight split at 800.7 us (forecast 795) and the front 8.9 later (forecast 8), but partly by luck. (820.85 less the forecast front of 803 is 18, so its own sum gives 18 and not 17.) The forecast took the turn-round of two buffers as what bounds the stretch; with eight buffers the splits end at 772.4 and the front still comes later, at 816.4. What the sum left out is that ACT's weight casts stand behind the copies of the maps, which waited 12.2 us for their load: between 766 and 778 us only one weight was cast.
- **The steady mLSTM (0; measured -6.1).** Put at 0 because its sequence of instructions is kept. It is, but the forecast did not see that the pair of before was locked to the grid of the clock. A pair other than 58.05 was among its own signs of being wrong.
- **The last chunks (5; measured 6.3).** The size is near by this border, but by that of the prediction's own row the gain is 0.6, so the term is not confirmed.
- **The first half of pass 1 (20; measured 17.1).** The size is right. 12.8 of it are the empty stretch, which is gone since the first operands are split ahead; the two blocks themselves became 4.3 us shorter. The rate is as in the working (295 GB/s, 296), so fewer bytes fit as well, but of the 35.2 us that these blocks still lose not all is volume. The stall at step 4, behind the weight split, came as described: a wait of 4.7 us, and a loss of 7.7 with 6.8 us at half clock around it, more than the 4 plus 1.7. The longest wait, 14.7 us, is another, and no term had it: in the second block ACT's cast of an operand that had landed at 1894.5 ran only at 1914.57. Ahead of it in ACT's queue stood the next load of a left operand, which waited for the transfer eight places ahead, a raw right operand of pass 2. SP issued that one at 1909.26, behind stores of sums that waited for POOL.

```profile
1914.57 1.04 ACT L104 CAST sr<-sr 128x1024 fp32r<-128x1024 f32 x1 [23.25 <-DMA xu<-in_w_in_dram]
```

- **Pass 2 (33; measured 5.3): the step that failed.** The forecast counted the time from a result to its transposes as a latency (it "now has two steps, 2 x 24 x 0.2263 = 10.9 us, where it had none or one") and left 17 of 50 us lost. The half statistics showed that DVE's work sets the pass: it is shorter by 19.8 us for 19.1 us of DVE work, while the transposes at other steps and the head norm tile by tile only moved the wait. That distance helps only where the engine that does the work has time in it fits both, but that DVE is full there remains argued. The forecast had DVE's share, 273.24 of 380.54, in its own table, and read an average. The second omission is smaller: the right sums of pass 3 were weighed as transfers ("8.4 MB"), not as four operations on POOL ahead of a power of 1 us. That is 8 to 9 us, by two runs. The waits for the scaling were to fall under 8 us; they are 24.0. Rival 3, with no gain in pass 2, fits this term better; it named loads and banks as the cause, where most of the waits are still the norm's, though the longest has a late skip load in it.
- **Pass 3 (6; measured -3.4).** The part on the weight splits held: the last block, where they stand, fell from 84.84 to 79.36 us. The first two blocks rose from 83.11 to 87.61 and from 76.16 to 79.91. The forecast did not price the left sums that now start there: with all three on DVE the second block is back at 76.16 and the pass 8.4 us shorter. The first block stays at 86.61 then, so its rise is not theirs; there TensorE waits for evictions (4.5 us in the pass) of transposes left over from pass 2, one of the prediction's signs of being wrong.
- **The start of pass 4 (14; measured 1.1).** The mechanism that was named came true: the loss at the step that waits for r fell from 18.0 to 6.1, where 5 were to be left. But a new wait of 11.5 us stands at the first step, and takes it back: the forecast moved three sums to a place where the first left split needs the same engine, and put their price at nothing.
- **The rivals.** The slower one (left loads that queue behind the sums' stores) did not show in its size: of its six blocks, the first two of pass 1 became 4.3 us shorter, and in the four of pass 2 the waits for a left cast (L104) are 1.1 us in all. Its mechanism is there once, in the wait of 14.7 us above. Rivals 1 and 2 would have left no gain at the start of pass 1 and at the entry, where 17.1 and 11.2 were found.
- **The range.** The deviations were taken as independent. Five of the six terms came out smaller, three of them for one reason: work was moved next to other work of the same engines, and its price there was put at zero.
